# Feed-forward tiles of a hybrid encoder: seven block products in three PSUM chains, two tiles interleaved

## The chip, the cores and the metric

The kernel runs on one core of one Trainium2 chip. The metric is the device time of one launch in microseconds (us). The kernel before was timed three times: 977.25, 977.26 and 977.32 us, median 977.26.

## The reference

The model is two layers deep and works on 512 frames of 1024 channels in float32. Layer 0 mixes the frames with a pooling mixer, layer 1 with chunked attention. Behind each mixer stands the same feed-forward, and that is the part the change touches:

```python
def conv_ffn(h, w_gate, w_val, conv_w, conv_b, w_out):
    a = h @ w_gate                                   # (512,1024) @ (1024,2816)
    ap = jnp.pad(a, ((0, 0), (CONV_W - 1, 0), (0, 0)))
    a = ap[:, 0:S] * conv_w[0] + ap[:, 1:S + 1] * conv_w[1] + ap[:, 2:S + 2] * conv_w[2] + conv_b
    return (jax.nn.silu(a) * (h @ w_val)) @ w_out    # (512,2816) @ (2816,1024)
```

For one layer this is called as `x + conv_ffn(rmsnorm(x, ffn_norm[i]), ...)`.

## The kernel before

**Tiles.** The 2816 hidden channels are cut into 22 tiles f of 128 channels. Every float32 operand is split into a high part (ScalarE writes it, line 98) and a low part (VectorE subtracts, line 99). A product of two such operands takes three matmuls: high by high, high by low, low by high (`mm3`, lines 119 to 121).

**Three kinds of tile** (`KIND`). Tiles 0 and 1 ("u") run early, on inputs that are not normalised yet. Tiles 2 to 4 ("p") are plain: gate and value, each over 8 pieces of 128 input channels. Tiles 5 to 21 ("s") go through `strassen`. There a tile's gate and value weights, each in two halves of 512 input channels, form a 2x2 block matrix (a11, a12 of the gate, a21, a22 of the value). The normalised input forms another 2x2 block matrix: b11, b12, b21, b22, by halves of the channels and of the frames. Seven products of 512 channels by 256 frames stand in place of eight. The weights are combined by four VectorE sums (lines 537 to 540) to s1 to s4; the input side has t1 to t4, made once per layer in `mixed`. The products are named after their input side: b11 (with a11), b21 (a12), t1 (s1), t2 (s2), b22 (s4), t3 (s3), t4 (a22). The results are

- gate, first half of the frames: b11 + b21
- gate, second half: b11 + t2 + t1 + b22
- value, first half: b11 + t2 + t3 + t4
- value, second half: b11 + t2 + t1 + t3

**Where the sums are made.** Each product has a PSUM bank of its own (tags S with four banks, P with two; Q has two for the output matmuls). b11 and t1 are copied to SBUF by ScalarE (line 561). All other additions are VectorE instructions that read one bank (lines 567 and 590) or SBUF alone (line 584).

**Narrow and wide products.** A narrow product is 4 times `mm3`: twelve matmuls of 256 columns. A wide product (`WIDE`) runs the high weights once over high and low input side by side, four matmuls of 512 columns (line 555), and then four of 256 columns for the low weights (line 557). The bank then holds two halves, and the second costs one more VectorE addition (line 563 or 567). Before, b11, t1 and t4 are wide in tiles 12 to 21.

**The order of the work.** TensorE's order is the program's own (`manual_schedule` for PE). All other engines get their order from a scheduler that runs a timeline of its own while the program is built; on the chip each engine then works through its list in order. `strassen` and `plain` are generators that stop after each product. Between two products the loop at lines 615 to 638 puts matmuls of `output`, the product of the group before with `w_out`: the tiles form four groups (`OUT`), and while one group's tiles are computed the group before is multiplied out, 2 to 4 output matmuls after each product, none after the first two products of a group (`WAIT`), and 54 kept back behind the last tile (`HOLD`). A tile's end is `hidden`: conv, silu, times value, split.

**Buffers that matter.** The parts of the weights go through a ring of three pairs of buffers (`ring`), four splits per tile. Raw weights arrive by DMA in three buffers. Tiles a, g and the sums sa and sb have 2, 6 and 2 buffers.

Of the kernel before, what the change touches and what calls it, by code (L numbers as in the profile page):

```python
# [18 lines left out]
F32R = mybir.dt.float32r  # L19
AF = mybir.ActivationFunctionType  # L20
# [3 lines left out]
P = 128  # L24
S = 512
# [3 lines left out]
NF = F // P  # L29
# [11 lines left out]
HALF = S // 2  # L41
# [9 lines left out]


KIND = "uuppp" + "s" * 17
WIDE = {f: ("b11", "t1", "t4") for f in range(12, NF)}
OUT = ((0, 5), (5, 6), (11, 6), (17, 5))
GM = 6
WAIT, HOLD = 2, 3
# [11 lines left out]
def trunk(ctx: ExitStack, tc: tile.TileContext, xt, xT, cols, band, edge, poolw, gv, wout, wqk, wv, wo, rel, out):  # L69
# [15 lines left out]
    def psum(tag, name, bufs=2):  # L85
        return ps.tile([P, S], F32, name=name, tag=tag, bufs=bufs)
# [3 lines left out]
    def g_tile(name):  # L90
        return tmp.tile([P, S], F32, name=name, tag="g", bufs=6)
# [22 lines left out]
        split(raw[:, :n], hi[:, :n], lo[:, :n], eng, eng_hi)  # L114
        return hi, lo

    def mm3(o, sh, sl, mh, ml, first, last):

        yield nc.tensor.matmul(o, sh, mh, start=first, stop=False)  # L119
        yield nc.tensor.matmul(o, sh, ml, start=False, stop=False)  # L120
        yield nc.tensor.matmul(o, sl, mh, start=False, stop=last)  # L121

    def run(steps):
        step = None
        for step in steps:
            pass
        return step
# [249 lines left out]
    def ffn(l, first, pool, acc, summed=None):  # L377
# [154 lines left out]
        def strassen(f):  # L532

            g, v = (raw_tile(f"gv{l}_{f}_{i}", gv[l, f, i]) for i in range(2))
            sa, sb = (sum_tile(f"s{x}{f}") for x in "ab")
            a11, a12, a21, a22, s1, s2, s4, s3 = (x[:, z * S:(z + 1) * S] for x in (g, v, sa, sb) for z in range(2))
            nc.vector.tensor_add(s1, a21, a22)
            nc.vector.tensor_sub(s2, s1, a11)
            nc.vector.tensor_sub(s3, a11, a21)
            nc.vector.tensor_sub(s4, a12, s2)  # L540

            def product(hl, z, name):


                nonlocal mm
# [4 lines left out]
                if name not in WIDE.get(f, ()):  # L550
                    for i, c in enumerate(cs):
                        mm = run(mm3(o[:, 0], hi[:, c], lo[:, c], B[i, name][:, 0], B[i, name][:, 1], i == 0, i == 3))
                    return [o[:, 0]]
                for i, c in enumerate(cs):
                    nc.tensor.matmul(o, hi[:, c], B[i, name], start=i == 0, stop=False)  # L555
                for i, c in enumerate(cs):
                    mm = nc.tensor.matmul(o[:, 0], lo[:, c], B[i, name][:, 0], start=False, stop=i == 3)
                return [o[:, 0], o[:, 1]]

            def copy(out, os):  # L560
                nc.scalar.activation(out, os[0], AF.Copy)
                for o in os[1:]:
                    nc.vector.tensor_add(out, o, out)

            def add(out, x, os):
                for o in os:
                    nc.vector.tensor_add(out, x, o)
                    x = out


            mm, banks = None, iter("SPSSPSS" if KIND[f - 1] == "s" else "PPSSSSS")
            a = pool.tile([P, S], F32, name=f"a{f}", tag="a", bufs=2)
            x, y, val = g_tile(f"x{f}"), g_tile(f"y{f}"), g_tile(f"v{f}")
            x1, x5, y6, y5 = x[:, :HALF], x[:, HALF:], y[:, :HALF], y[:, HALF:]
# [15 lines left out]
            nc.vector.tensor_add(val.rearrange("p (h s) -> p h s", h=2), y.rearrange("p (h s) -> p h s", h=2), o)  # L590
# [4 lines left out]
            yield mm  # L595

        def output(g):

# [13 lines left out]
        with tc.manual_schedule(engines={mybir.EngineType.PE}):  # L612
            h, seed, known, made = early()
            queue, left, n = [], 0, 0
            for g, (b, m) in enumerate(OUT):
                steps = {"s": 7, "p": 8, "u": 0}
                points = sum(steps[KIND[f]] for f in range(b, b + m))
                hold = HOLD * 3 * OUT[g - 1][1] if g == len(OUT) - 1 else 0
                todo, at = left, 0
                for f in range(b, b + m):  # L620
                    if KIND[f] == "u":
                        continue
                    for mm in (strassen if KIND[f] == "s" else plain)(f):
                        at += 1
                        if n in range(3, 20, 5):
                            with tc.issue_after(made.ins):
                                mixed(h, n // 5)
                        n += 1
                        if at > WAIT:
                            due = (todo - hold) * (at - WAIT) // (points - WAIT)  # L630
                            while todo - left < due:
                                next(queue[0])
                                left -= 1
# [337 lines left out]
```

## Time and profile before

| | |
|---|---|
| median of three timed runs | 977.26 us |
| span of the profiled execution, first to last instruction | 975.1 us |
| TensorE busy | 967.0 us, 5582 matmuls |
| VectorE busy | 807.8 us, 1468 instructions |
| ScalarE busy | 541.4 us, 926 instructions |
| TensorE on the chain that ended last | 94% |
| mean granted TensorE clock | 1.000 |

The page gives no other time for the profiled execution than its span; the median of the timed runs lies 2.2 us above it. In the profile's rows st_b and st_t are the banks of the seven products, out the bank of the output matmuls, g_h and g_l the high and low part of a tile's weights, ow_h and ow_l those of `w_out`, two, one and h the parts of the input. A matmul's row shows a modelled duration that overlaps the next one, so the pace of TensorE is read from start to start.

### The profile page before, as it was taken

What the parts mean: (1) busy time and instruction counts of PE and PEld (TensorE: products, weight loads), DVE (VectorE), ACT (ScalarE), POOL (GpSimd) and SP (SyncE); (2) the same over time, 40 slices, a digit from 0 to 9 for tenths busy, and PEclk for the clock granted to TensorE, in tenths of its full rate; (3) what the DMA queues carried; (4) which work ended last, traced back from release to release, by engine and by line L of the source; (5) the groups of instructions that cost most, each with busy time, mean ns of one, the idle gap of its engine ahead of it and who ended that gap; (6) DMA issues with size and microseconds to landing.
All of it is one profiled execution on the core that took longest, in us unless ns stands there. A gap on an engine that the chain in (4) does not pass through costs nothing.

```text
span 975.1 us, 15058 instructions
## 1 busy us (share of the span) xinstructions
PE 967.0 (99%) x5582; PEld 847.0 (87%) x5582; DVE 807.8 (83%) x1468; ACT 541.4 (56%) x926; POOL 103.2 (11%) x90
## 2 busy tenths in 40 slices
PE   9999999999999999999999999999999999999998
PEld 8788999998899888888888787888999989899986
DVE  8999989999999854442777887999989998999953
ACT  7665454544454544345898988656545444455421
POOL 2300000000000013204534442000000000000000
PEclk9999999999999999999999999999999999999999
DMA  9222323333333234232333341232333333233323
GB/s 341 70 85 71 117 89 111 119 113 98 104 92 103 68 90 150 89 119 96 112 114 105 96 118 54 87 110 79 104 110 118 92 105 111 86 117 98 100 71 111
DMA packets 37433, 102.91 MB, mean 106 GB/s; under 512 B 4432, under 2 KB 7904, under 8 KB 37360
## 3 DMA queue, kind: packets, MB, share of 16 engines
q1 hardware_dynamic: 37296, 101.90, 33.7%
q8 instruction: 44, 0.72, 0.3%
q14 instruction: 29, 0.24, 0.1%
q0 software_dynamic: 32, 0.04, 0.0%
q10 hardware_dynamic: 32, 0.00, 0.0%
HBM read 95.60 MB, written 2.14 MB: 100 GB/s over the span
## 4 chain that ended last, share of the span: by engine, by line
PE 94%; DVE 4%; ACT 2%; issue 0%; DMA 0%; DVEq 0%; ACTq 0%
PE out L120 8%; PE out L119 8%; PE out L121 8%; PE st_t L120 5%; PE st_t L119 5%; PE st_t L121 5%; PE st_b L120 4%; PE st_b L119 4%; PE st_b L121 4%; PE st_t L555 4%; PE gv L120 4%; PE gv L119 4%; PE gv L121 4%; PE qk L120 3%; PE qk L119 3%; PE qk L121 3%
## 5 line engine op out<-in xcount | busy, mean ns | idle before, releaser
L98 ACT ACTIVATE g_h<-gv_r 128x1024 fp32r<-128x1024 f32 x68 | 57.7, 848 | 79.2 <-PE st_t L120 37.5
L120 PE MATMUL out<-one,ow_h 128*128 128x512 f32 x224 | 88.1, 393 | 0.0
L119 PE MATMUL out<-one,ow_h 128*128 128x512 f32 x224 | 87.8, 392 | 0.0
L121 PE MATMUL out<-one,ow_l 128*128 128x512 f32 x224 | 87.7, 392 | 0.0
L98 ACT ACTIVATE ow_h<-wo_r 128x640 fp32r<-128x640 f32 (+1 forms) x64 | 50.5, 789 | 59.6 <-PE out L120 47.0
L608 DVE TENSOR_TENSOR X<-out,X 128x512 f32<-128x512 f32 (+1 forms) x65 | 43.9, 677 | 38.1 <-PE out L121 37.8
L98 ACT ACTIVATE g_h<-sa 128x1024 fp32r<-128x1024 f32 x34 | 36.1, 1060 | 59.1 <-PE st_t L120 42.4
L99 DVE TENSOR_TENSOR g_l<-gv_r,g_h 128x1024 fp32r<-128x1024 f32 x68 | 64.6, 950 | 4.8 <-ACT g_h L98 4.5
L99 DVE TENSOR_TENSOR ow_l<-wo_r,ow_h 128x640 fp32r<-128x640 f32 (+1 forms) x64 | 56.5, 882 | 0.0
L419 DVE SCALAR_TENSOR_TENSOR c<-a,col,c 128x511 f32<-128x511 f32 (+1 forms) x76 | 56.2, 742 | 0.1
L120 PE MATMUL st_t<-h,g_h 128*128 128x256 f32 x192 | 54.3, 283 | 0.0
L119 PE MATMUL st_t<-h,g_h 128*128 128x256 f32 x192 | 54.3, 283 | 0.0
L121 PE MATMUL st_t<-h,g_l 128*128 128x256 f32 x192 | 54.3, 283 | 0.0
L121 PE MATMUL st_t<-two,g_l 128*128 128x256 f32 x192 | 54.0, 281 | 0.0
L120 PE MATMUL st_t<-two,g_h 128*128 128x256 f32 x192 | 53.9, 281 | 0.0
L119 PE MATMUL st_t<-two,g_h 128*128 128x256 f32 x192 | 53.8, 280 | 0.0
L121 PE MATMUL qk<-wqk_h,two 128*128 128x512 f32 x128 | 51.4, 402 | 0.0
L119 PE MATMUL qk<-wqk_h,two 128*128 128x512 f32 x128 | 50.8, 409 | 0.0
L120 PE MATMUL qk<-wqk_l,two 128*128 128x512 f32 x128 | 50.8, 397 | 0.0
L121 PEld LDWEIGHTS out<-one,ow_l 128*128 128x128 f32 x224 | 42.3, 189 | 6.6
L119 PEld LDWEIGHTS out<-one,ow_h 128*128 128x128 f32 x224 | 42.4, 189 | 5.9
L120 PEld LDWEIGHTS out<-one,ow_h 128*128 128x128 f32 x224 | 42.5, 190 | 5.3 <-DVE one L99 0.2
(331 smaller groups left out, 3154.3 us busy)
## 6 DMA issues: line engine op xcount, KB each, us to landing
gv_r<-gv SPq DMA_DIRECT2D x86, 512.0 KB, 3.6
wo_r<-wout SPq DMA_DIRECT2D x32, 384.0 KB, 3.1
wo_r<-wout SPq DMA_DIRECT2D x32, 320.0 KB, 2.9
wqk_r<-wqk SPq DMA_DIRECT2D x16, 512.0 KB, 3.5
wv_r<-wv SPq DMA_DIRECT2D x8, 512.0 KB, 3.5
wo_r<-wo SPq DMA_DIRECT2D x8, 512.0 KB, 3.5
xt<-xt SPq DMA_DIRECT2D x4, 512.0 KB, 5.2
X<-xT SPq DMA_DIRECT2D x8, 256.0 KB, 7.5
```

The costliest lines, as they stand in the source:

```text
L98: nc.scalar.activation(hi, raw, AF.Copy)
L99: return (eng or nc.vector).tensor_sub(lo, raw, hi.bitcast(F32))
L119: yield nc.tensor.matmul(o, sh, mh, start=first, stop=False)
L120: yield nc.tensor.matmul(o, sh, ml, start=False, stop=False)
L121: yield nc.tensor.matmul(o, sl, mh, start=False, stop=last)
L419: nc.vector.scalar_tensor_tensor(c[:, j:], a[:, :S - j], cw[2 - j], c[:, j:], op0=OP.mult, op1=OP.add)
L555: nc.tensor.matmul(o, hi[:, c], B[i, name], start=i == 0, stop=False)
L608: nc.vector.tensor_add(X[d][:, fs], o[:, fs], X[d][:, fs])
```

## The change

A tile's sums are now chained in PSUM. The bank "main" takes b11, then t2 on top of it, then t1, then b22; after each of the four links ScalarE copies the bank's first half out to where that partial sum is wanted (b11 to the gate's first half, b11 + t2 to the value's first half, plus t1 to the value's second half, plus b22 to the gate's second half). The bank "b" takes b21. The bank "t" takes t3 and later, on top of it, t4. VectorE adds b21, t3 and t3 + t4 to the copies. The next link may not write the main bank before ScalarE has read it, and t4 may not write its bank before VectorE has read t3.

The products come in another order (b11, b21, t2, t3, t1, b22, t4), the weight sums share their tiles in other pairs (s2 with s3 in sa, s1 with s4 in sb), and the last two products of a tile run between the first products of the next tile: b11 of f+1, b22 of f, b21 of f+1, t4 of f, t2 of f+1, and so on. a22 is split into two g tiles instead of the ring, so the ring has three splits per tile. Wide are now b21, t3, t4 and b22, in tiles 9 to 21: 13 tiles x 4 products x 2 layers = 104 wide products against 10 x 3 x 2 = 60.

```diff
-WIDE = {f: ("b11", "t1", "t4") for f in range(12, NF)}
+WIDE = {f: ("b21", "t3", "t4", "b22") for f in range(9, NF)}
...
-            a11, a12, a21, a22, s1, s2, s4, s3 = (x[:, z * S:(z + 1) * S] for x in (g, v, sa, sb) for z in range(2))
+            a11, a12, a21, a22, s2, s3, s1, s4 = (x[:, z * S:(z + 1) * S] for x in (g, v, sa, sb) for z in range(2))
...
+            def bank(tag, name):
+                return psum(tag, f"st{l}_{f}_{name}", 4 if tag == "S" else 2).rearrange("p (c n) -> p c n", c=2)
+
+            def product(o, hl, z, name, first):
                 hi, lo = hl
-                tag = next(banks)
-                o = psum(tag, f"st{l}_{f}_{name}", 4 if tag == "S" else 2).rearrange("p (c n) -> p c n", c=2)
                 cs = [slice((4 * z + i) * P, (4 * z + i + 1) * P) for i in range(4)]
...
+            def add(x, o, both):
+                for c in range(2 if both else 1):
+                    nc.vector.tensor_add(x, x, o[:, c])
+
+            def copy(x, o):
+                nc.scalar.activation(x, o[:, 0], AF.Copy)
...
-            copy(x1, product(w, 0, "b11"))
-            yield mm
-            add(a[:, :HALF], x1, product(w, 1, "b21"))
-            yield mm
+            main, side = bank("S", "m"), bank("P", "b")
+            product(main, w, 0, "b11", True)
+            copy(a[:, :HALF], main)
+            yield
+            product(side, w, 1, "b21", True)
+            add(a[:, :HALF], side, "b21" in wide)
+            yield
             w = parts(sa, 1024, f"g2_{f}")
-            copy(x5, product(w, 0, "t1"))
-            yield mm
-            add(y6, x1, product(w, 1, "t2"))
-            nc.vector.tensor_add(y5, y6, x5)
-            yield mm
+            product(main, w, 0, "t2", False)
+            copy(val[:, :HALF], main)
+            yield
+            side = bank("S", "t")
+            product(side, w, 1, "t3", True)
+            yield
             w = parts(sb, 1024, f"g3_{f}")
-            add(a[:, HALF:], y5, product(w, 0, "b22"))
-            yield mm
-            o = product(w, 1, "t3")[0][:, None, :].to_broadcast([P, 2, HALF])
-            nc.vector.tensor_add(val.rearrange("p (h s) -> p h s", h=2), y.rearrange("p (h s) -> p h s", h=2), o)
-            w = parts(a22, 512, f"g4_{f}")
-            yield mm
-            add(val[:, :HALF], val[:, :HALF], product(w, 0, "t4"))
+            last = [tmp.tile([P, S], F32R, name=f"g4_{f}_{c}", tag="g", bufs=6) for c in "hl"]
+            split(a22, *last)
+            product(main, w, 0, "t1", False)
+            copy(val[:, HALF:], main)
+            add(val[:, HALF:], side, "t3" in wide)
+            yield
+            product(main, w, 1, "b22", False)
+            copy(a[:, HALF:], main)
+            if "b22" in wide:
+                nc.vector.tensor_add(a[:, HALF:], a[:, HALF:], main[:, 1])
+            yield
+            product(side, last, 0, "t4", False)
+            add(val[:, :HALF], side, "t4" in wide)
             hidden(f, a, lambda c: nc.vector.tensor_mul(c, val, c))
...
+                if KIND[f] == "s":
+                    mine = [(f, j) for j in range(5)]
+                    order += [x for j in range(2) for x in (mine[j], (prev, 5 + j))] + mine[2:] if prev else mine
+                    prev = f
+            order += [(prev, 5), (prev, 6)]
```

**VectorE at tile 5 of layer 0**, the first Strassen tile, where the plain tiles 3 and 4 are still being finished (c_818 and c_898 are their conv results, t_... and h_... the mixed input blocks of `mixed`, sa and sb the weight sums). Before, the low part of sa, `g_5_l<-sa_910`, stood ahead of all of this:

```order
L99 TENSOR_TENSOR g_5_l<-sa_910,g_5_h 128x1024
L499 TENSOR_TENSOR t_3_851<-hl_587,t_3_851 128x256
L419 SCALAR_TENSOR_TENSOR c_898<-gv_4_0_832,col,c_898 128x511
L419 SCALAR_TENSOR_TENSOR c_818<-gv_3_0_742,col,c_818 128x510
L99 TENSOR_TENSOR h_470<-t_2_797,h_470 128x512
L539 TENSOR_TENSOR sb_911<-gv_5_0_r,gv_5_1_r 128x512
L540 TENSOR_TENSOR sb_911<-gv_5_0_r,sa_910 128x512
L501 TENSOR_TENSOR t_3_852<-hl_587,t_3_851 128x256
L419 SCALAR_TENSOR_TENSOR c_898<-gv_4_0_832,col,c_898 128x510
L99 TENSOR_TENSOR h_473<-t_3_851,h_473 128x512
L567 TENSOR_TENSOR a_916<-x_917,st_5_b_938 128x256
L529 TENSOR_TENSOR c_818<-gv_3_1_783,c_818 128x512
```

In the changed kernel the same stretch reads:

```order
L538 TENSOR_TENSOR sa_910<-sb_911,gv_5_0_r 128x512
L539 TENSOR_TENSOR sa_910<-gv_5_0_r,gv_5_1_r 128x512
L501 TENSOR_TENSOR t_3_852<-hl_587,t_3_851 128x256
L419 SCALAR_TENSOR_TENSOR c_898<-gv_4_0_832,col,c_898 128x510
L99 TENSOR_TENSOR h_473<-t_3_851,h_473 128x512
L529 TENSOR_TENSOR c_818<-gv_3_1_783,c_818 128x512
L540 TENSOR_TENSOR sb_911<-gv_5_0_r,sa_910 128x512
L563 TENSOR_TENSOR a_916<-a_916,st_5_b 128x256
L99 TENSOR_TENSOR g_5_l<-sa_910,g_5_h 128x1024
L99 TENSOR_TENSOR h_474<-t_3_852,h_474 128x512
```

The split of sa moved from the head of the stretch to behind the addition of product b21 (`a_916<-a_916,st_5_b`), which waits for TensorE. In layer 1 the same split comes behind line 529's product of tile 3, but ahead of that addition.

**ScalarE at tile 14.** Before, two copies out of PSUM (line 561, x) stand among the splits:

```order
L98 ACTIVATE g_14_h<-gv_14_0_r 128x1024
L98 ACTIVATE ow_1_4_h<-wo_1_4_r 128x768
L98 ACTIVATE g_14_h<-sa_2408 128x1024
L417 ACTIVATE c_2392<-a_2253,col 128x512
L98 ACTIVATE g_14_h<-sb_2409 128x1024
L561 ACTIVATE x_2415<-st_14_b_2422 128x256
L98 ACTIVATE ow_1_5_h<-wo_1_5_r 128x768
L420 ACTIVATE c_2392<-c_2392 128x512
L98 ACTIVATE g_14_h<-gv_14_1_r 128x512
L98 ACTIVATE u2h<-c_2392 128x512
L561 ACTIVATE x_2415<-st_14_t_2466 128x256
```

Now there are four per tile (line 566; a and v, tiles 13 and 14 in turn, out of their main banks):

```order
L566 ACTIVATE a_2259<-st_14_m 128x256
L98 ACTIVATE g_14_h<-sb_2254 128x1024
L566 ACTIVATE a_2107<-st_13_m 128x256
L98 ACTIVATE g_15_h<-gv_15_0_r 128x1024
L417 ACTIVATE c_2327<-a_2107,col 128x512
L566 ACTIVATE v_2339<-st_14_m 128x256
L98 ACTIVATE g_14_h<-gv_14_1_r 128x512
L420 ACTIVATE c_2327<-c_2327 128x512
L98 ACTIVATE g_15_h<-sa_2412 128x1024
L566 ACTIVATE v_2339<-st_14_m 128x256
L98 ACTIVATE u2h<-c_2327 128x512
L98 ACTIVATE ow_1_5_h<-wo_1_5_r 128x768
```

Each copy now stands behind a weight split or behind a step of the tile before, and TensorE waits for three of the four. In TensorE's order the distance between the end of a link and the next link of the same bank is, in products and output matmuls between them: b11 to t2 four products in most tiles (one product in tile 5); t2 to t1 the product t3 with 5 to 8 output matmuls, but without any in tiles 11 and 17; t1 to b22 the next tile's b11 with 5 to 8 output matmuls, but only three output matmuls and no product in tile 21. The order of the attention part and of the pooling part is the same on every engine. SyncE issues the same DMAs; some loads of `w_out` stand one to three places later among the loads of gate and value weights.

More of the change, by code (lines that the diff above doesn't have):

```diff
@@ L115, in load_split, with mm3 @@
         return hi, lo
[L117 to L121, printed above, removed]
+    def mm3(o, sh, sl, mh, ml, first, last, **how):
+        yield nc.tensor.matmul(o, sh, mh, start=first, stop=False, **how)
+        yield nc.tensor.matmul(o, sh, ml, start=False, stop=False, **how)
+        yield nc.tensor.matmul(o, sl, mh, start=False, stop=last, **how)
     def run(steps):
@@ L540, in strassen @@
             nc.vector.tensor_sub(s4, a12, s2)
-            def product(hl, z, name):
-                nonlocal mm
+            wide = WIDE.get(f, ())
+            def bank(tag, name):
+                return psum(tag, f"st{l}_{f}_{name}", 4 if tag == "S" else 2).rearrange("p (c n) -> p c n", c=2)
+            def product(o, hl, z, name, first):
                 hi, lo = hl
-                tag = next(banks)
-                o = psum(tag, f"st{l}_{f}_{name}", 4 if tag == "S" else 2).rearrange("p (c n) -> p c n", c=2)
@@ L549, in product @@
                 cs = [slice((4 * z + i) * P, (4 * z + i + 1) * P) for i in range(4)]
-                if name not in WIDE.get(f, ()):
+                how = {"skip_group_check": not first}
+                if name not in wide:
                     for i, c in enumerate(cs):
-                        mm = run(mm3(o[:, 0], hi[:, c], lo[:, c], B[i, name][:, 0], B[i, name][:, 1], i == 0, i == 3))
-                    return [o[:, 0]]
+                        run(mm3(o[:, 0], hi[:, c], lo[:, c], B[i, name][:, 0], B[i, name][:, 1], first and i == 0, i == 3, **how))
+                    return
@@ L554, in product @@
                 for i, c in enumerate(cs):
-                    nc.tensor.matmul(o, hi[:, c], B[i, name], start=i == 0, stop=False)
+                    nc.tensor.matmul(o, hi[:, c], B[i, name], start=first and i == 0, stop=False, **how)
                 for i, c in enumerate(cs):
[L557 to L571, printed above, removed]
+                    nc.tensor.matmul(o[:, 0], lo[:, c], B[i, name][:, 0], start=False, stop=i == 3, **how)
+            def add(x, o, both):
[3 more added lines that the diff above has]
+                nc.scalar.activation(x, o[:, 0], AF.Copy)
@@ L592, in strassen @@
[L592 to L593 removed]
+            product(main, w, 0, "b11", True)
[4 more added lines that the diff above has]
+            yield
+            val = g_tile(f"v{f}")
+            w = parts(sa, 1024, f"g2_{f}")
+            product(main, w, 0, "t2", False)
+            copy(val[:, :HALF], main)
+            yield
+            side = bank("S", "t")
@@ L594, in strassen @@
+            yield
+            product(side, last, 0, "t4", False)
+            add(val[:, :HALF], side, "t4" in wide)
             hidden(f, a, lambda c: nc.vector.tensor_mul(c, val, c))
-            yield mm
+            yield
         def output(g):
@@ L614, in ffn @@
             queue, left, n = [], 0, 0
+            order, prev = [], None
+            for f in range(NF):
+                if KIND[f] == "p":
+                    order += [(f, j) for j in range(8)]
+                if KIND[f] == "s":
[3 more added lines that the diff above has]
+            order += [(prev, 5), (prev, 6)]
+            steps = {f: (plain if KIND[f] == "p" else strassen)(f) for f, _ in order}
+            ends = [max(x for x, (f, _) in enumerate(order) if f == b + m - 1) + 1 for b, m in OUT]
             for g, (b, m) in enumerate(OUT):
-                steps = {"s": 7, "p": 8, "u": 0}
-                points = sum(steps[KIND[f]] for f in range(b, b + m))
+                begin = ends[g - 1] if g else 0
+                points = ends[g] - begin
                 hold = HOLD * 3 * OUT[g - 1][1] if g == len(OUT) - 1 else 0
[L619 to L633, printed above, removed]
+                todo = left
+                for at, (f, _) in enumerate(order[begin:ends[g]], 1):
+                    next(steps[f])
+                    if n in range(3, 20, 5):
+                        with tc.issue_after(made.ins):
+                            mixed(h, n // 5)
+                    n += 1
+                    if at > WAIT:
+                        due = (todo - hold) * (at - WAIT) // (points - WAIT)
+                        while todo - left < due:
+                            next(queue[0])
+                            left -= 1
                 if g:
```

2 lines of the change are left out of this document (removed).

## The prediction

> **What bounds the kernel now.** I read the busy times first.
>
> ```profile
> PE 967.0 (99%) x5582; PEld 847.0 (87%) x5582; DVE 807.8 (83%) x1468; ACT 541.4 (56%) x926; POOL 103.2 (11%) x90
> ```
>
> A matmul's row overlaps the next, so 99% may hide pauses. I therefore asked for TensorE's own waits, in the whole span:
>
> ```profile
> PE warm L201 <- POOL ident masks.py:199: 1.4, 1, 1.4
> PE wo L120 <- DVE two L99: 0.7, 1, 0.7
> PE oo L814 <- DVE pt1l L99: 0.5, 1, 0.5
> PE tp L802 <- ACT sb L794: 0.5, 2, 0.3
> PE y L285 <- ACT two L224: 0.4, 1, 0.4
> PE po L119 <- DVE one L104: 0.3, 1, 0.3
> ```
>
> Those are all, 3.8 us, and no line of the feed-forward is among them. The stage view shows two Strassen stretches of layer 0 (columns: stretch, its length, then busy time and count of PE, PEld, DVE, ACT, POOL):
>
> ```profile
> core 0: us, PE busy (x) PEld busy (x) DVE busy (x) ACT busy (x) POOL busy (x), PEclk, DMA share, GB/s
> 86.00:186.00 100.00, 100.00 (x712) 94.08 (x711) 94.50 (x150) 50.87 (x75) 0.00 (x0) 1.00 0.34 104
> 186.00:270.00 84.00, 84.00 (x524) 75.69 (x524) 77.32 (x126) 40.29 (x57) 0.00 (x0) 1.00 0.34 104
> ```
>
> TensorE never stops there; VectorE is at 92 to 94%, ScalarE near half. So the feed-forward costs what TensorE's matmuls cost. Work taken from VectorE gains nothing by itself; fewer or cheaper matmuls gain, and every new wait of TensorE is paid in full.
>
> **Part 1: more wide products (gain).** The timeline of TensorE has a wide product (line 555), a narrow one (119 to 121) and a wide one directly behind each other; 861.01 is an output matmul:
>
> ```profile
> 861.01 0.40 PE L121 MATMUL out<-one,ow_l 128*128 128x512 f32 x1
> 861.24 0.62 PE L555 MATMUL st_b<-two,g_h 128*128 128x512 f32 x2
> ...
> 862.62 0.28 PE L119 MATMUL st_b<-two,g_h 128*128 128x256 f32 x1
> ...
> 864.06 0.63 PE L555 MATMUL st_t<-two,g_h 128*128 128x512 f32 x2
> ...
> 865.46 0.40 PE L119 MATMUL out<-u0h,ow_h 128*128 128x512 f32 x1
> ```
>
> From start to start the wide ones take 1.38 and 1.40 us, the narrow one 1.44, an output matmul 0.23. Both kinds stream 3072 columns; the wide one needs 8 matmuls for it instead of 12. The difference lies between 0.04 and 0.06 us in these rows. The change makes 104 - 60 = 44 more products wide: 44 x 0.04 = 1.8 us to 44 x 0.06 = 2.6. I take 1.8: these rows show times in steps of 0.01, and the two narrow products of tile 5 (below) take 2.87 together, 1.435 each, 0.035 to 0.055 above the wide ones.
>
> The Trainium skill ("TensorE: Matmul & The Clock Gate", section "Back-to-back issue gap") speaks against this gain: a warm matmul costs its columns at 2.4 GHz plus a fixed 2.5 ns, so four matmuls fewer would save 10 ns per product and 44 of them an estimated 0.4 us. The rows disagree: 0.04 us for four matmuls is 10 ns for each.
>
> **Part 2: tile 5, layer 0 (cost).** The second product on the main bank, t2, starts third in tile 5, where t1 started before: it needs the low part of sa from its third matmul on.
>
> ```profile
> 86.12 0.28 PE L119 MATMUL st_b<-two,g_h 128*128 128x256 f32 x1
> ...
> 88.99 0.28 PE L119 MATMUL st_t<-two,g_h 128*128 128x256 f32 x1
> 89.11 0.28 PE L120 MATMUL st_t<-two,g_h 128*128 128x256 f32 x1
> 89.23 0.28 PE L121 MATMUL st_t<-two,g_l 128*128 128x256 f32 x1
> ```
>
> So it is wanted at 89.23. VectorE has no pause in this stretch of its timeline:
>
> ```profile
> 83.83 1.21 DVE L99 TENSOR_TENSOR g_l<-sa,g_h 128x1024 fp32r<-128x1024 f32 x1
> ...
> 89.42 0.68 DVE L99 TENSOR_TENSOR h<-t,h 128x512 fp32r<-128x512 f32 x1
> 90.02 0.41 DVE L567 TENSOR_TENSOR a<-x,st_b 128x256 f32<-128x256 f32 x1
> 90.35 0.68 DVE L529 TENSOR_TENSOR c<-gv,c 128x512 f32<-128x512 f32 x1
> ```
>
> An instruction starts 0.08 before the one ahead has ended (90.02 against 89.42 + 0.68). Before, the split ran at 83.83. Now it stands behind the addition on b21. That addition ran at 90.02; the split (1.21 - 0.08 = 1.13) is no longer ahead of it, line 529 (0.68 - 0.08 = 0.60) newly is: 90.02 - 1.13 + 0.60 = 89.49. The split follows 0.33 later (90.35 - 90.02) and ends at 89.82 + 1.21 = 91.03. TensorE stands from 89.23 to then, 1.8 us; with 0.1 for the signal, an estimate, 1.9. Below: even an idle VectorE must wait for b21's end, which is t2's start (88.99) plus some 0.16 of the last matmul's tail (0.28 - 0.12), so the split ends at 90.69 at the earliest: 1.5. Above: another 0.68 in front, 2.6. Nothing hides it, since behind t2 TensorE's own list is fixed.
>
> **Part 3: tile 5, layer 1 (cost).** There the split is behind line 529 but ahead of the addition.
>
> ```profile
> 678.78 1.21 DVE L99 TENSOR_TENSOR g_l<-sa,g_h 128x1024 fp32r<-128x1024 f32 x1
> ...
> 683.32 0.67 DVE L529 TENSOR_TENSOR c<-gv,c 128x512 f32<-128x512 f32 x1
> 683.92 0.40 DVE L567 TENSOR_TENSOR a<-x,st_b 128x256 f32<-128x256 f32 x1
> ```
>
> ```profile
> 683.61 0.28 PE L121 MATMUL st_t<-two,g_l 128*128 128x256 f32 x1
> ```
>
> The place where line 567 started, 683.92, comes 1.13 earlier and is now the split's: 682.79 to 684.00, wanted at 683.61. 0.4 us; bounds 0 and 1.1 (one 0.68 more in front).
>
> **Part 4: the chain's waits.** ScalarE's copies out of PSUM and the split that may be ahead of one:
>
> ```profile
> L98 ACT ACTIVATE g_h<-sa 128x1024 fp32r<-128x1024 f32 x34 | 36.1, 1060 | 59.1 <-PE st_t L120 42.4 <-issue 12.2 <-DVE sa L538 3.0
> ...
> L561 ACT ACTIVATE x<-st_t 128x256 f32<-128x256 f32 x34 | 13.0, 383 | 37.2 <-PE st_t L557 22.3 <-PE st_t L121 14.8
> L561 ACT ACTIVATE x<-st_b 128x256 f32<-128x256 f32 x34 | 13.0, 383 | 33.1 <-PE st_b L557 20.7 <-PE st_b L121 12.4
> ```
>
> ```profile
> 862.82 0.38 ACT L561 ACTIVATE x<-st_b 128x256 f32<-128x256 f32 x1 [1.66 <-PE st_b L557]
> ```
>
> The bank's product ended where the next began, at 862.62. ScalarE, idle, copied from 862.82 to 863.20: the bank is free 0.58 after the link, or 0.58 + 1.06 = 1.64 if a split has just begun. The next link comes later than that nearly everywhere: with t3 (1.39) and five to eight output matmuls (0.23 each) 2.5 to 3.2 us. At these links I take nothing, and their cover is 0.9 us even behind a split. In tiles 11 and 17 of both layers t2 to t1 has only t3, and b11 to t2 of tile 5 only b21: 1.4 us. Nothing if ScalarE is free, 0.24 behind a split, six times, at most 1.4. In tile 21 t1 to b22 has three output matmuls, 0.69: with the signal 0.1 each, 0.2 for two layers; behind a split 1.06 each, 2.1.
>
> The Trainium skill ("PSUM — Partial Sum Buffer", section "Summary: rules for kernel authors") says that an engine should read another bank than the one TensorE is writing. The chain goes against that, and the price would be the whole of those 0.58 us at each of three links in 34 tiles, an estimated 59 us, if TensorE had nothing to do in other banks. It has.
>
> **Part 5: VectorE and ScalarE.** The adds of a tile:
>
> ```profile
> L590 DVE TENSOR_TENSOR v<-y,st_t 128x512 f32<-128x512 f32 x34 | 23.1, 681 | 6.0 <-PE st_t L121 5.6
> L567 DVE TENSOR_TENSOR v<-v,st_t 128x256 f32<-128x256 f32 x54 | 22.2, 412 | 0.1
> ```
>
> A narrow tile had five of 0.41 and one of 0.68, 2.7 us, a wide one three more, 4.0. Now it is three (1.2) or seven (2.9). Per layer 7 x 2.7 + 10 x 4.0 = 58.9 becomes 4 x 1.2 + 13 x 2.9 = 42.5: VectorE loses 33 us in two layers and TensorE, which did not wait for it, gains nothing. ScalarE gets two copies of 0.38 per tile, 26 us in all, at half load. The ring's three splits per tile, the a22 split in g tiles and the later loads of w_out lengthen no distance that TensorE waits for: zero.
>
> **Sum.** -1.8 + 1.9 + 0.4 + 0.2 = +0.7 us. The profiled span 975.1 becomes 975.8; the timed runs stand 2.2 above the span, so 978.0. Bounds: -2.6 + 1.5 = -1.1 and -1.5 (44 x 0.035) + 2.6 + 1.1 + 1.4 + 2.1 = +5.7.
>
> **The rivals.**
> *The copies hold TensorE (slower).* In ScalarE's list the copy of t2 stands behind the conv start of the tile before, which waits for a VectorE addition. If that comes late, the copy misses the 2.5 to 3.2 us window. It decides once ScalarE reaches the copy more than 1.9 us (2.5 - 0.58) after the link; 0.2 to 0.5 us lost in each of 34 tiles is 7 to 17 us, 985 to 995. For it: VectorE at 94%, and a list made by a scheduler's clock. Against: the addition has a lead of some 6 us (three products, nine to twelve output matmuls).
> *Four matmuls fewer save less (slower).* The 0.04 us may belong to what stands beside the products in these rows rather than to their matmul count. If a quarter is left (0.01 x 44 = 0.4), the sum is -0.4 + 1.9 + 0.4 + 0.2 = +2.1, 979.4. Against: the 1.435 of tile 5 has other neighbours. The rule of the Trainium skill in part 1 would have it so.
> *The wide products give more (same or faster).* With 0.06 each and the smallest stalls -1.1, 976.2; past that, 0.08 each would give 975.2.
> *VectorE was the bound (faster).* Then up to 33 us come back, 944. For: 94% busy. Against: no wait of TensorE for it. That the change does nothing of what it says is out: the lists show it.
>
> **How the numbers follow.** A measurement of this kernel can tell about 0.2%, 1.95 us, from no change. Forecast 0.64 (0.60 within 1.95 us, 0.04 above), copies 0.20, smaller saving 0.06, larger 0.07 (0.03 same, 0.04 faster), VectorE 0.03. Same 0.63, slower 0.30, faster 0.07. The range leaves out the far parts of the first and last rival and takes the sum's bounds nearly whole: 976.0 to 982.0.
>
> **What would show it.** Right: in layer 0 a wait of TensorE of 1.5 to 2.6 us at tile 5's t2 for the split of sa, a smaller one in layer 1; line 557 and 559's products at 1.39 us; hardly a wait for line 566's copies apart from tile 21. Wrong: waits for line 566 in many tiles, a wide product under 1.35, or no pause at tile 5.

## The result, and the profile after

The changed kernel takes 979.04 us (median of 10 runs, 978.75 to 980.45); the kernel before, timed beside it, 977.29 us (977.02 to 977.53, 10 runs). The ratio is 1.0019, 95% interval 1.0011 to 1.0028: slower by 1.8 us, a little under the 1.95 us within which the prediction called a result no change. The profiled execution took 978.75 us, its span is 977.0 (before 975.1).

The busy times of the changed kernel:

```profile
PE 966.9 (99%) x5406; PEld 837.7 (86%) x5406; DVE 780.5 (80%) x1410; ACT 560.2 (57%) x994; POOL 103.0 (11%) x90
```

VectorE lost 27 us, ScalarE gained 19, TensorE lost 176 matmuls, and the kernel is not faster. TensorE's waits in the whole span (columns: us in total, times, longest) show two lines that were not there before:

```profile
PE st_m L121 <- DVE g_l L99: 1.7, 2, 1.5
...
PE out L119 <- ACT ow_h L98: 0.3, 1, 0.3
```

The first is the pause at t2 of tile 5, in both layers. This view counts a pause from the modelled end of the matmul ahead, so the whole loss is read from start to start. TensorE's timeline at tile 5, first layer 0, then layer 1:

```profile
86.20 0.28 PE L119 MATMUL st_m<-two,g_h 128*128 128x256 f32 x1
...
88.95 0.28 PE L121 MATMUL st_b<-h,g_l 128*128 128x256 f32 x1
89.22 0.39 PE L119 MATMUL st_m<-two,g_h 128*128 128x256 f32 x1
89.44 0.28 PE L120 MATMUL st_m<-two,g_h 128*128 128x256 f32 x1
91.18 0.39 PE L121 MATMUL st_m<-two,g_l 128*128 128x256 f32 x1 [1.46 <-DVE g_l L99]
...
681.83 0.28 PE L119 MATMUL st_m<-two,g_h 128*128 128x256 f32 x1
...
684.82 0.28 PE L120 MATMUL st_m<-two,g_h 128*128 128x256 f32 x1
685.37 0.39 PE L121 MATMUL st_m<-two,g_l 128*128 128x256 f32 x1 [0.28 <-DVE g_l L99]
```

A matmul of 256 columns normally starts 0.12 us after the one before. In layer 0 the steps from 88.95 on are 0.27, 0.22 and 1.74, and 0.22 behind the pause: together 1.97 us too long. The first of these is late because ScalarE finished the high part of sa only at 89.16; that costs nothing of its own, since the low part came later still. In layer 1 the loss is 0.43 + 0.10, about 0.54. VectorE's timeline has the cause, in the order that the lists showed:

```profile
88.98 0.68 DVE L540 TENSOR_TENSOR sb<-gv_r,sa 128x512 f32<-128x512 f32 x1
89.58 0.41 DVE L563 TENSOR_TENSOR a<-a,st_b 128x256 f32<-128x256 f32 x1
89.91 1.21 DVE L99 TENSOR_TENSOR g_l<-sa,g_h 128x1024 fp32r<-128x1024 f32 x1
```

The second line of the waits was not forecast. TensorE, VectorE and ScalarE in layer 1:

```profile
707.70 0.40 PE L121 MATMUL out<-one,ow_l 128*128 128x512 f32 x1
708.40 0.50 PE L119 MATMUL out<-u0h,ow_h 128*128 128x512 f32 x1 [0.30 <-ACT ow_h L98]
```

```profile
703.98 0.69 DVE L99 TENSOR_TENSOR g_l<-gv_r,g_h 128x512 fp32r<-128x512 f32 x1
```

```profile
707.61 0.74 ACT L98 ACTIVATE ow_h<-wo_r 128x640 fp32r<-128x640 f32 x1 [1.40 <-DMA wo_r<-wout]
```

The split of a22 (VectorE, until 704.67) is the last reader of a raw weight buffer. The load of `w_out` into that buffer was issued at 704.70 and landed at 707.59; ScalarE split it at once; TensorE waited from 707.93 (an output matmul takes 0.23) to 708.40 and lost 0.1 more behind it: 0.57 us. At two other waits for a load of `w_out` 0.08 us went at 752.4 and 0.02 at 157.7. There the load followed the sum s4 (line 540), the last reader of the gate's raw buffer: it ended at 748.59, and the load was issued at 748.65.

Where the 1.85 us lie, by the start of tile 5's b11 (before: 86.12 above in the prediction, and in layer 1 this row):

```profile
680.50 0.28 PE L119 MATMUL st_b<-two,g_h 128*128 128x256 f32 x1
```

| stage | before | after | difference | pauses added | 22 more wide products |
|---|---|---|---|---|---|
| start to tile 5 of layer 0 | 86.12 | 86.20 | +0.08 | | |
| from there to tile 5 of layer 1 | 594.38 | 595.63 | +1.25 | 1.97 + 0.13 | -0.88 |
| from there to the end | 294.62 | 295.14 | +0.52 | 0.54 + 0.57 + 0.13 | -0.88 |

The 0.13 are single places under 0.1 us: t1 of tile 5, t1 to b22 of tile 21 (0.04 in each layer) and `w_out`. A wide product takes 1.389 us from start to start (median of 104), a narrow one 1.429 (median of 134 traced whole): 0.040 for each.

### The profile page after: what moved, and what is told of

It is laid out like the page before. It is cut to its first block, busy times and chain, and to the rows that moved or that the text cites. A ratio compares the mean times of both kernels' runs of the same rounds, so it can differ in the third digit from the quotient of the medians.

```text
span 977.0 us, 14625 instructions
## 1 busy us (share of the span) xinstructions
PE 966.9 (99%) x5406; PEld 837.7 (86%) x5406; DVE 780.5 (80%) x1410; ACT 560.2 (57%) x994; POOL 103.0 (11%) x90
## 4 chain that ended last, share of the span: by engine, by line
PE 88%; DVE 8%; ACT 2%; DMA 1%; issue 1%; DVEq 0%; ACTq 0%
PE out L119 8%; PE out L120 8%; PE out L121 8%; PE st_m L121 5%; PE st_m L120 5%; PE st_t L557 5%; PE st_m L119 5%; PE qk L120 3%; PE qk L119 3%; PE qk L121 3%; PE gv L120 3%; PE gv L119 3%; PE gv L121 3%; PE st_t L559 3%; PE st_m L557 2%; PE st_b L557 2%
## 5 line engine op out<-in xcount | busy, mean ns | idle before, releaser
L566 ACT ACTIVATE v<-st_m 128x256 f32<-128x256 f32 x68 | 26.0, 382 | 120.3 <-PE st_m L121 120.2
L98 ACT ACTIVATE g_h<-gv_r 128x512 fp32r<-128x512 f32 (+1 forms) x68 | 57.2, 842 | 22.2 <-PE st_b L557 14.5
L99 DVE TENSOR_TENSOR g_l<-gv_r,g_h 128x512 fp32r<-128x512 f32 (+1 forms) x68 | 64.6, 950 | 4.1 <-ACT g_h L98 4.1
L99 DVE TENSOR_TENSOR g_l<-sb,g_h 128x1024 fp32r<-128x1024 f32 x34 | 41.6, 1223 | 28.5 <-ACT g_h L98 28.5
L121 PE MATMUL st_m<-two,g_l 128*128 128x256 f32 x220 | 62.2, 283 | 1.7 <-DVE g_l L99 1.7
L119 PE MATMUL st_m<-h,g_h 128*128 128x256 f32 x220 | 62.2, 283 | 0.0
L121 PE MATMUL st_m<-h,g_l 128*128 128x256 f32 x220 | 62.2, 283 | 0.0
L120 PE MATMUL st_m<-h,g_h 128*128 128x256 f32 x220 | 62.2, 283 | 0.0
L120 PE MATMUL st_m<-two,g_h 128*128 128x256 f32 x220 | 61.9, 281 | 0.0
L119 PE MATMUL st_m<-two,g_h 128*128 128x256 f32 x220 | 61.7, 281 | 0.0
L563 DVE TENSOR_TENSOR v<-v,st_t 128x256 f32<-128x256 f32 x120 | 49.4, 412 | 2.3 <-ACT v L566 2.0
L98 ACT ACTIVATE g_h<-sb 128x1024 fp32r<-128x1024 f32 x34 | 36.0, 1059 | 22.8 <-PE st_m L557 15.0
```

The lines of the kernel that those rows point to most:

```text
L98: nc.scalar.activation(hi, raw, AF.Copy)
L99: return (eng or nc.vector).tensor_sub(lo, raw, hi.bitcast(F32))
L119: yield nc.tensor.matmul(o, sh, mh, start=first, stop=False, **how)
L120: yield nc.tensor.matmul(o, sh, ml, start=False, stop=False, **how)
L121: yield nc.tensor.matmul(o, sl, mh, start=False, stop=last, **how)
L563: nc.vector.tensor_add(x, x, o[:, c])
```

## The experiments

Ratios are to the kernel before on the same chip in the same session.

### The changed kernel again

> The changed kernel once more, beside the three kernels below. If its 979.0 us belong to the kernel, it gives 978.7 to 979.6 and the same pauses as before: 1.9 us at tile 5 of layer 0, 0.5 us at tile 5 of layer 1, and about 0.55 us in layer 1 before the second output column block of the group (a wait for the high part of w_out). If that last pause hangs on how long one transfer happens to take, it differs from run to run, and with it the time, by up to some 0.7 us.

979.61 us (978.95 to 981.82, 11 runs), ratio 1.0023 (1.0014 to 1.0032). The pauses at tile 5 are 1.97 and 0.55 us again. Those before `w_out` are others than in the first profile: 0.19 at 157.6, 0.32 at 708.1, 0.46 at 752.4. So these waits change from run to run, and the runs spread over 2.9 us, those of the kernel before over 1.2. The length of the transfer changed little: from issue to split the three loads took 2.88 to 2.97 us in the first profile and 2.95 to 2.99 here. What changed more is the moment of issue against TensorE's arrival: at 708 the load was issued 0.12 us later and TensorE came 0.41 us later.

### The sums of tile 5 in another buffer

The reason why the split of sa came late lies further up VectorE's list. sa and sb of tile 5 take over two buffers that hold the input blocks ha and hb while `mixed` runs. The buffer goes to whichever tile is written first. VectorE's list of the changed kernel, with row numbers:

```
108 L500 TENSOR_TENSOR t_1_750<-hl_585,ha 128x256
115 L537 TENSOR_TENSOR sb_911<-gv_5_1_r 128x512
129 L500 TENSOR_TENSOR t_3_852<-hl_587,hb 128x256
134 L538 TENSOR_TENSOR sa_910<-sb_911,gv_5_0_r 128x512
```

Before, s1 and s2 shared sa, and s1 came first, so sa followed the last reader of ha. Now s1 is in sb; sb takes ha's place, and sa has to wait for the last reader of hb, row 129. The edit makes s2 and s3 without s1 and adds s1 anew behind them:

```diff
...
+            if f == 5:
+                nc.vector.tensor_add(s2, a21, a22)
+                nc.vector.tensor_sub(s2, s2, a11)
+                nc.vector.tensor_sub(s3, a11, a21)
+                nc.vector.tensor_add(s1, a21, a22)
...
```

> Tile 5 alone: s2 and s3 are made without s1, so that their tile sa takes the buffer that is free first; s1 is then added a second time into sb (one VectorE addition more per layer). In VectorE's list the split of sa now stands ahead of the addition of b21, as in the kernel before. My theory: the two pauses at tile 5 are all that this place costs, 1.9 + 0.5 us, so the time falls by 2.0 to 2.6 us, to 976.4 to 977.0, and the trace shows no wait of TensorE at t2 of tile 5; the pause at w_out stays. Rival: VectorE is full in this stretch, and whatever is put first only pushes another split (sb's, or a mixed block) behind the moment it is wanted; then the time falls by less than 1 us and a new wait stands at t3, t1 or the next tile's b11.

982.89 us (982.41 to 983.97, 5 runs), ratio 1.0056 (1.0043 to 1.0068). My theory of the time fell. That of the buffer held: the split of sa now starts at 84.54, ahead of the addition of b21. The pause at t2 for it is gone, and others stand in its place:

```profile
PE st_t L120 <- DVE h L99: 2.1, 1, 2.1
...
PE st_m L119 <- DVE c L419: 1.2, 1, 1.2
...
PE st_m L119 <- ACT a L572: 0.5, 1, 0.5
```

b11 of tile 5 now waits for the conv of tile 3 (line 419), which frees its PSUM bank; t2 for the copy of b11, which stands behind ScalarE's split; and in layer 1 t3 for a mixed block (h), by 2.3 us. The rival was right: VectorE is full here, and what is put first pushes something else too late. It was right by more than it said, since the long pause cost a second time (last section).

### a22 split earlier, and both edits

```diff
+            last = [tmp.tile([P, S], F32R, name=f"g4_{f}_{c}", tag="g", bufs=6) for c in "hl"]
+            split(a22, *last)
             product(side, w, 1, "b21", True)
...
```

The same two lines go out ahead of t1.

> In all Strassen tiles the split of a22 is written ahead of the product b21 instead of ahead of t1, so that the raw weight buffer comes free earlier and the next load of w_out can start earlier. My theory: the 0.55 us pause in layer 1 comes from that buffer; it goes, and the time falls by 0.4 to 0.8 us to 978.2 to 978.6, with a smaller spread between runs than the 1.7 us seen of the changed kernel. Rival one: the load stands behind the gate and value loads in SyncE's list and is no earlier, so nothing changes. Rival two: the earlier split takes VectorE's time ahead of the split of sa in tile 5, or holds two g tiles longer, and the time rises by 0.5 to 1 us.

980.95 us (980.62 to 982.42, 5 runs), ratio 1.0038 (1.0025 to 1.0050). The waits before `w_out` are gone, as my theory had it: with a22 split earlier, a raw buffer comes free earlier. But the time rises by rival two:

```profile
90.36 0.28 PE L120 MATMUL st_m<-two,g_h 128*128 128x256 f32 x1
92.69 0.39 PE L121 MATMUL st_m<-two,g_l 128*128 128x256 f32 x1 [2.05 <-DVE g_l L99]
```

The pause at t2 grew from 1.74 to 2.33 us in layer 0 and from 0.55 to 1.16 in layer 1, and a wait of 0.5 us for a copy came at 691.2. Less the 0.67 us saved before `w_out`, these make about 1.1 of the 2.2 us by which this profile's span (979.2) exceeds the changed kernel's. Another 0.9 lies in the first 8.3 us, where TensorE waits 0.76 us for a split by ScalarE (line 224); nothing in the edit touches that stage, and why it came late stays open.

> The edits of e1 and e2 together. My theory: the two savings add up, 2.4 to 3.2 us less than the changed kernel, 975.8 to 976.6, which is the kernel before less the 1.7 to 1.8 us of the 44 wide products, and 0.7 to 1.5 us under the kernel before. Rival: the chain itself (four links on one bank, ScalarE's copies) costs something spread over all tiles that single pauses don't show; then this kernel stays at 977.3 or above although the pauses are gone.

983.42 us (981.51 to 983.87, 5 runs), ratio 1.0057 (1.0043 to 1.0071): the pauses of the first edit, with 3.0 us at t3 of layer 1. Neither theory was tested, since the pauses did not go away.

### The split of sa ahead of two instructions, then sb ahead of tile 6

The next two kernels change no instruction, only places in the lists. In the first, the split of sa comes ahead of s4 and of the addition of b21 (`tc.issue_after(x)` keeps an instruction behind x):

```diff
...
+                w1, w2 = parts(g, 1024, f"g1_{f}"), parts(sa, 1024, f"g2_{f}", later=True)
+                low, high = w2[2](), parts.high
+            with tc.issue_after(low.ins) if f == 5 else nullcontext():
+                nc.vector.tensor_sub(s4, a12, s2)
...
+            with tc.issue_after(high.ins) if f == 5 else nullcontext():
+                copy(a[:, :HALF], main)
...
+            with tc.issue_after(low.ins) if f == 5 else nullcontext():
+                add(a[:, :HALF], side, "b21" in wide)
...
```

> Only three places of the lists change at tile 5: ScalarE makes the high part of sa ahead of its copy of b11, and VectorE makes the low part ahead of s4 (line 540) and of the addition of b21; nothing else is moved and no instruction is added. Theory one, a single late split: the split starts at 88.98 behind line 529 and ends at 90.19 instead of 91.12, the pause at t2 of layer 0 falls from 1.9 to about 0.8 us, that of layer 1 goes, and the time falls by 1.1 to 1.5 us to about 977.6 to 978.4. Theory two, VectorE as the bound of the stretch: everything behind the addition keeps its old time, the low part of sb still ends at about 95.2 while t1 now wants it 1.1 us earlier, so the pause only moves from t2 to t1 and the time falls by less than 0.5 us, to 978.9 or above.

979.61 us (978.52 to 981.56, 6 runs), ratio 1.0027 (1.0016 to 1.0039): nothing gained. VectorE and TensorE of this kernel in layer 0:

```profile
89.10 1.21 DVE L406 TENSOR_TENSOR g_l<-sa,g_h 128x1024 fp32r<-128x1024 f32 x1
...
91.77 1.21 DVE L99 TENSOR_TENSOR g_l<-gv_r,g_h 128x1024 fp32r<-128x1024 f32 x1
...
94.11 1.22 DVE L99 TENSOR_TENSOR g_l<-sb,g_h 128x1024 fp32r<-128x1024 f32 x1
```

```profile
89.36 0.28 PE L120 MATMUL st_m<-two,g_h 128*128 128x256 f32 x1
90.37 0.38 PE L121 MATMUL st_m<-two,g_l 128*128 128x256 f32 x1 [0.73 <-DVE g_l L406]
...
94.36 0.28 PE L120 MATMUL st_m<-two,g_h 128*128 128x256 f32 x1
95.38 0.38 PE L121 MATMUL st_m<-two,g_l 128*128 128x256 f32 x1 [0.73 <-DVE g_l L99]
```

This is theory two: half of the pause stays at t2, and the other half stands at t1, which waits for the low part of sb. In layer 1 the pause moved to t1 whole and grew from 0.54 to 0.92 us. Ahead of that split VectorE does the first split of tile 6 (91.77), which tile 6 wants only from 97.4 on. The second kernel puts it behind (`parts.ahead` are the two halves of the split of sb of tile 5):

```diff
...
+                for x in parts.ahead if f == 6 else ():
+                    after.enter_context(tc.issue_after(x.ins))
...
```

> The edit of e10, and the split of sb of tile 5 ahead of the first split of tile 6 on both engines. Theory two: the low part of sb ends 1.1 us earlier, at about 94.1, and t1 no longer waits; the first split of tile 6 ends at 95.2 and is wanted at about 96.4. Then only 0.8 us are left at t2 of layer 0 and the time is about 1.2 to 1.6 us under the changed kernel, 978.0 to 978.4; under e10 by about 1 us. If theory one is right, e11 is equal to e10.

976.79 us (976.70 to 976.96, 11 runs), ratio 0.9995 (0.9986 to 1.0004): 2.3 us under the changed kernel's 979.04, more than I expected, and the spread is 0.3 us. The two splits now stand in the other order:

```profile
92.97 1.21 DVE L406 TENSOR_TENSOR g_l<-sb,g_h 128x1024 fp32r<-128x1024 f32 x1
94.11 1.21 DVE L99 TENSOR_TENSOR g_l<-gv_r,g_h 128x1024 fp32r<-128x1024 f32 x1
```

Besides tile 21 (0.04 in each layer) one pause of the feed-forward is left, 0.99 us from start to start:

```profile
PE st_m L121 <- DVE g_l L406: 0.7, 1, 0.7
```

The waits before `w_out` are gone too, without an edit for them: in layer 1 VectorE has done a22 by 701.99 instead of 704.67 and the load lands at 704.93. Of the 2.8 us between this profile's span and the one ahead, the pauses at t1 are 0.99 and 0.92 and the waits before `w_out` 0.77.

The edit names two splits, but the scheduler answered it by moving about a dozen other VectorE instructions of tiles 6 to 8 in each layer. That bears on `w_out`. In the changed kernel VectorE stood idle for 1.06 us ahead of this row, because a sum that waits for a weight load headed its list:

```profile
700.04 0.69 DVE L537 TENSOR_TENSOR sb<-gv_r 128x512 f32<-128x512 f32 x1 [1.06 <-DMA gv_r<-gv]
```

Here a split (697.97) and an addition (699.11) that do not wait stand ahead of that sum. So the gain at t1 belongs to the two splits; how much of the gain at `w_out` is theirs and how much is the scheduler's new order is not shown.

### The rest of the pause, and two more wide tiles

```diff
...
+                tc.add_manual_dep(plain.last[3].ins, low.ins.name, mybir.DependencyInfo(mybir.DependencyClass.NoSync, mybir.DependencyReason.DATA), reason="issue_after")
...
```

> The edits of e11, and VectorE's product of tile 3 (line 529) behind the low part of sa as well, in both layers. If the pause of 0.9 us that is left at t2 of layer 0 is that instruction and nothing else, it falls by 0.60 us to about 0.3, and the time falls from 976.8 to 976.2 (976.0 to 976.4). Rival: the product frees the PSUM bank that t3 writes; 0.6 us later it holds t3 instead, and the time stays at 976.8.

976.81 us (976.50 to 977.78, 11 runs), ratio 0.9995 (0.9986 to 1.0004). Once more the pause was divided, not shortened:

```profile
89.44 0.28 PE L120 MATMUL st_m<-two,g_h 128*128 128x256 f32 x1
89.90 0.39 PE L121 MATMUL st_m<-two,g_l 128*128 128x256 f32 x1 [0.17 <-DVE g_l L406]
...
93.90 0.28 PE L120 MATMUL st_m<-two,g_h 128*128 128x256 f32 x1
94.37 0.39 PE L121 MATMUL st_m<-two,g_l 128*128 128x256 f32 x1 [0.19 <-DVE g_l L406]
```

The rival named t3 as the place; it is t1 again.

```diff
-WIDE = {f: ("b21", "t3", "t4", "b22") for f in range(9, NF)}
+WIDE = {f: ("b21", "t3", "t4", "b22") for f in range(7, NF)}
```

> The edits of e13, and the same four products wide in tiles 7 and 8 too: 120 wide products in place of 104. If TensorE is the bound there, 16 x 0.038 = 0.6 us less than e13, 975.4 to 975.8. Rival: VectorE is still full in tiles 5 to 8, and 16 more additions of 0.41 us put a split behind the moment it is wanted; then the time is no better than e13, or worse by up to a few us.

976.44 us (975.97 to 977.16, 11 runs), ratio 0.9991 (0.9982 to 1.0000). It is the lowest time of all kernels, 0.9 us under the kernel before; the interval just reaches no difference. Against the kernel without these two wide tiles it is 0.4 us, not the 0.6 forecast, and the runs of the two overlap, so a gain from them is not shown.

### Without wide products, and more of them in the old structure

```diff
-WIDE = {f: ("b21", "t3", "t4", "b22") for f in range(9, NF)}
+WIDE = {}
```

> The changed kernel with no wide product at all: 104 products of twelve matmuls in place of eight, so 416 matmuls more, and 104 VectorE additions fewer. My theory: 0.038 us for each product, 4.0 us, 983.0 to 983.7. Rival: the saving of four matmuls is a matter of the neighbours and a quarter of that, 1 us, 980.4 or less.

985.36 us (983.05 to 988.20, 5 runs), ratio 1.0084 (1.0068 to 1.0099), above both forecasts. The 104 products take 1.43 us each now, so of the 6.6 us between the two spans 104 x 0.040 = 4.2 are theirs. Most of the rest is one wait at an ordinary link, t1 to b22 of tile 14 in layer 1, on TensorE and ScalarE:

```profile
831.19 0.39 PE L119 MATMUL out<-one,ow_h 128*128 128x512 f32 x1
833.09 0.39 PE L119 MATMUL st_m<-two,g_h 128*128 128x256 f32 x1 [1.51 <-ACT v L566]
```

```profile
831.92 0.84 ACT L98 ACTIVATE ow_h<-wo_r 128x768 fp32r<-128x768 f32 x1 [2.48 <-DMA wo_r<-wout]
832.67 0.37 ACT L566 ACTIVATE v<-st_m 128x256 f32<-128x256 f32 x1
```

ScalarE stood idle for a load of `w_out`; the copy that TensorE waited for stood behind that split. So the chain can hold TensorE, by way of a late transfer; in the changed kernel it happened not to.

Next, the kernel before with the wider set of wide products and nothing else:

```diff
-WIDE = {f: ("b11", "t1", "t4") for f in range(12, NF)}
+WIDE = {f: ("b11", "b21", "t1", "t4") for f in range(9, NF)}
```

> The kernel before, but with b11, b21, t1 and t4 wide in tiles 9 to 21: 104 wide products in the old structure, without chains or interleaving. My theory: TensorE is the bound there and the 44 products give their 1.7 us, 975.6 to 976.0, if VectorE keeps pace. Rival: VectorE, at 92 to 94 per cent in these stretches, gets 44 more additions of 0.41 us (18 us) in the tiles from 9 on, falls behind and holds TensorE; then the time is above 977.4, and only the fewer additions of the chain make room for the wide products.

982.47 us (981.61 to 983.88, 5 runs), ratio 1.0056 (1.0043 to 1.0068): the rival. The products do take 1.39 us, but VectorE falls behind:

```profile
PE out L120 <- DVE one L99: 3.0, 2, 1.5
PE out L119 <- ACT one L98: 1.7, 1, 1.7
```

In this profile, too, 0.9 us went in the first 8 us, as in the kernel with a22 earlier. The three waits alone are 4.7 us. In the old structure VectorE has no room for the wide products; the chain's fewer additions are what they stand on.

### The chain under load

Both are made on top of the kernel at 976.79. First, every copy out of the main bank is made twice:

```diff
                 nc.scalar.activation(x, o[:, 0], AF.Copy)
+                nc.scalar.activation(x, o[:, 0], AF.Copy)
```

> The edits of e11, and each of ScalarE's four copies per tile made twice in a row, so that a link's bank is free about 0.3 us later at every link; 136 more instructions of 0.38 us on ScalarE. My theory: at an ordinary link the next link comes 2.5 to 3.2 us later and 0.58 + 0.3 us fit, in tiles 11 and 17 (1.4 us) also; only in tile 21 it shows, 0.3 us in each layer. The time rises from 976.8 by 0.3 to 1.0 us, to 977.1 to 977.8. Rival, the copies hold TensorE: each link is paid, some 100 links x 0.3 us, and the time rises by 10 to 30 us.

985.52 us (984.11 to 986.92, 4 runs), ratio 1.0082 (1.0068 to 1.0096). The rise of 8.7 us lies between the two theories. Most ordinary links stay free or lose 0.1; tile 5 and tile 21 lose 0.4 to 0.6 at single links. The most, 2.0 us in layer 0 and 2.3 in layer 1, is lost between t1 and b22 of tile 13. That is an ordinary link, with a product and three output matmuls in between, and not one of the short windows of tiles 11 and 17. There a split of `w_out` that waits for its load and the copies stand in each other's way in ScalarE's list; the last of the losses is the link itself:

```profile
219.05 0.50 PE L561 MATMUL st_m<-two,g_h 128*128 128x512 f32 x1 [0.53 <-ACT v L571]
```

Then the last two products of a tile go directly behind its first five:

```diff
-                    order += [x for j in range(2) for x in (mine[j], (prev, 5 + j))] + mine[2:] if prev else mine
-                    prev = f
-            order += [(prev, 5), (prev, 6)]
+                    order += mine + [(f, 5), (f, 6)]
```

> The edits of e11, but the last two products of a tile run directly behind its first five, without the next tile's b11 and b21 between them. From t1 to b22 there are then only output matmuls (0.5 to 1.2 us) in every tile, as it is in tile 21. My theory: the copy needs 0.58 us if ScalarE is idle and up to 1.64 us behind a split, so waits of 0.1 to 1 us for line 570's copy appear in many of the 34 tiles, 5 to 15 us in all, 982 to 992. Rival: ScalarE is idle nearly always at that moment, and the time rises by less than 2 us; then the interleaving buys nothing.

991.62 us (991.04 to 992.09, 4 runs), ratio 1.0144 (1.0130 to 1.0158), as my theory had it. TensorE now waits on the chain in many tiles:

```profile
PE st_t L561 <- DVE v L567: 2.9, 5, 1.0
PE st_m L561 <- ACT v L570: 2.8, 6, 0.8
PE st_m L119 <- ACT v L570: 2.0, 4, 0.7
```

The first line is t4, which follows t3 in its bank and waits for VectorE to read it. The two products of the next tile are the cover of the chain; without them the kernel takes 15 us more.

## Why the prediction was right, and where it was not

**Wide products.** 1.8 us forecast, 44 x 0.040 = 1.76 measured, and without any wide product all 104 take the 1.43 us of a narrow one. Four matmuls fewer save 10 ns each here, so both rivals on this saving, a smaller and a larger one, are out. The Trainium skill ("TensorE: Matmul & The Clock Gate", section "Back-to-back issue gap") does not stand against this as far as part 1 had it: it gives the 2.5 ns for a single matmul by itself, and says that at small column counts this under-counts a stream of weight loads and matmuls.

**Tile 5.** 1.9 us forecast in layer 0, 1.97 measured; the split was to end at 91.03 and ended at 91.12. The 0.1 for the signal was an estimate that names no row; TensorE started 0.06 behind the split's end, and the step behind the pause was 0.1 too long. In layer 1 it was 0.4 and 0.54. The mechanism was right for the list as it stood. What the step did not see: the place in the list is a consequence of the buffer that sa takes over, and the loss is set by all of VectorE's work up to t1. Two experiments show it: with the split of sa moved alone, layer 0 loses 0.99 at t2 and 0.99 at t1, as much as before; with both splits moved it loses 0.99 at t2 and nothing at t1.

**Chain waits.** 0 at ordinary links, as forecast; tile 21 cost 0.04 us per layer instead of 0.1. That they are free because of the interleaving was argued in the prediction and shown by the kernel without it. Nor does ScalarE read the bank that TensorE is writing, as part 4 says of the chain: the next link waits for the copy. That not one ordinary link paid was in part luck. With the same chain, the kernel without wide products lost 1.8 us at one of them, where a split that waited for its load of `w_out` stood ahead of the copy; part 4 reckoned with splits ahead of a copy, but not with their loads.

**What failed** is the last sentence of part 5: "the a22 split in g tiles and the later loads of w_out lengthen no distance that TensorE waits for: zero". It was 0.67 us in the profiled execution and 0.97 in the second profile. I had looked at the places of the loads in SyncE's list, not at when their buffers come free.

**VectorE and ScalarE.** Part 5 had VectorE lose 33 us and ScalarE gain 26; it was 27 and 19. The counts behind them were right (58 instructions fewer, 68 more), but 33 and 26 are sums of row durations, and each row's last 0.08 to 0.1 us lies under the next row. Neither is a term of the sum.

**The sum.** -1.76 + 1.97 + 0.54 + 0.09 + 0.67, and 0.06 at t1 of tile 5, is +1.6; the span grew by 1.85. About 0.1 is the start, and some 0.2 are spread over the attention part and single matmuls and stay unexplained. The median came out 1.0 above the forecast, chiefly by the term of `w_out`.

**VectorE was the bound.** I gave it 0.03, since TensorE had no wait for it. As a bound on the whole that holds: 27 us less on VectorE brought nothing by themselves. In tiles 5 and 6 of each layer, and in the old structure with 104 wide products, it holds TensorE all the same. A view of before in stretches of 4 us would have shown it, with TensorE and VectorE both full from 78 to 114:

```profile
86.00:90.00 4.00, 4.00 (x35) 3.96 (x34) 4.00 (x8) 1.88 (x5) 0.00 (x0) 1.00 0.10 16
...
106.00:110.00 4.00, 4.00 (x31) 3.79 (x30) 4.00 (x7) 1.64 (x3) 0.00 (x0) 1.00 0.35 109
```

## What to carry to other kernels

A TensorE that never waits may have an engine beside it that never rests either: look at that engine in short stretches. Ask what the next wanted result behind a moved instruction is, because a pause that is taken away in one place reappears at the next deadline unless the work between them shrinks or its order changes. When tiles are paired in another way, check which earlier buffer each one takes over and who reads that last. When an edit moves two instructions, compare the whole list, since the scheduler may move others. A chain in one PSUM bank costs next to nothing as long as other products lie between its links, but it makes TensorE depend on whatever stands ahead of the copy in ScalarE's list, transfers included.

## What the runs showed of the hardware

A pause of TensorE can cost twice. In the kernel with s2 made first, at t3 of layer 1 two matmuls start 2.39 us apart, and from about 1 us behind the pause the matmuls come every 0.21 us in place of 0.12 for some 3.4 us; the granted clock in the stretch view (last but two column) shows it:

```profile
688.59 0.28 PE L119 MATMUL st_t<-h,g_h 128*128 128x256 f32 x1
690.98 0.38 PE L120 MATMUL st_t<-h,g_h 128*128 128x256 f32 x1 [2.11 <-DVE h L99]
...
692.34 0.41 PE L121 MATMUL st_m<-two,g_l 128*128 128x256 f32 x1
692.55 0.41 PE L119 MATMUL st_m<-two,g_h 128*128 128x256 f32 x1
```

```profile
688.00:692.00 4.00, 1.89 (x13) 1.57 (x12) 4.00 (x6) 1.23 (x3) 0.00 (x0) 1.00 0.00 0
692.00:696.00 4.00, 4.00 (x19) 3.74 (x18) 3.74 (x6) 1.46 (x2) 0.00 (x0) 0.57 0.31 94
696.00:700.00 4.00, 4.00 (x30) 3.74 (x29) 1.18 (x3) 1.64 (x4) 0.00 (x0) 1.00 0.74 252
```

The matmuls from 692.13 to 695.66 take 1.5 us longer than at full clock, on top of the 2.3 of the pause. The pause of 3.0 us in the kernel with both edits did the same (granted clock 0.60 from 692 to 696). Of that kernel's five runs, four have a mean clock of 0.997 or 0.998 and take 983.2 to 983.9 us; the fifth has 1.000 and takes 981.5. The pause of 2.33 us in the kernel with a22 earlier did not lower the clock in its profiled execution. Nor did two steps of 2.12 and 2.00 us one behind the other, at 783 to 787 in the profiled execution of the old structure with more wide products; but two other runs of that kernel have a mean clock of 0.996 and take 2 us more, and no trace shows where. The Trainium skill ("TensorE: Matmul & The Clock Gate", section "HAM oscillation — how this bites in real kernels") warns of gaps over some 3.4 us. Here 2.4 were enough; 0.3 us of other pauses lay 6 us ahead, and no run shows whether they mattered.
